# Encoder block in 32-bit floats: three of five units of the down projection by seven products, accumulators of one bank, running sums of squares

## The chip, the cores and the metric

The kernel runs on one core of a Trainium2 chip. The metric is the device time of one execution in microseconds (us); of several runs the median counts.

A core has a matrix engine (TensorE, in profiles PE, its weight loads PEld), a vector engine (VectorE, DVE), a scalar engine (ScalarE, ACT), GpSimd (POOL) and SyncE (SP), which here issues the transfers (DMA). Each engine works through its own list of instructions in order and waits on semaphores for the others. Matmuls write into eight accumulator banks of 128 x 512 floats.

## The reference

One layer of an encoder on x (256 tokens x 2048), all in 32-bit floats, cut to its steps:

```python
hn = rmsnorm(h, mix_norm_pre)
z, xbc, dt_raw, u = split(hn @ w_in)                    # 2048 -> 3616 columns
y_ssd  = ssd_mixer(z, xbc, dt_raw, ...)                 # state space mixer, both directions, 16 heads
y_pool = pool_mixer(u, pool_w, pool_scale)              # means over windows of 2, 4, 8, 16
h = h + rmsnorm(concat(y_ssd, y_pool) @ w_out, mix_norm_post)
hn = rmsnorm(h, ffn_norm_pre)
gate, val = split(hn @ w_up)                            # 2048 -> 2 x 5632
ff = (gelu(dwconv(gate)) * val) @ w_down                # 5632 -> 2048
h = h + rmsnorm(ff, ffn_norm_post)
gate = sigmoid(rmsnorm(h, ple_norm_pre) @ w_gate)       # 2048 -> 2048
h = h + rmsnorm(gate * (p @ w_ple), ple_norm_post)      # p: 256 tokens x 256
```

Every rmsnorm divides a row by the root of its mean square, so the whole row has to be known before the first element of the result.

## The kernel before

**The products.** Each weight tile is loaded raw (four buffers), cast to a rounded high part by ScalarE (`whi`) and subtracted from it by VectorE (`wlo`, the low part); five buffers each. A product of 32-bit floats is then three matmuls: high x high, high x low, low x high. The activations are held in the same two parts, as panels with the channels on the partitions.

**The stages in order.** The first projection columns (dt and u, accumulators `dtu`), then three slabs of `xbc`, then `z`, then w_out (`wo`), then for each of 11 slabs of 512 columns gate (`ga`) and value (`va`), then w_down (`dn`), then w_gate (`gt`). The small product `ple` with w_ple (24 matmuls a half) runs between w_out and gate, and between down and w_gate. Loads are issued by SP in the order of the program; within one engine a scheduler has fixed the order of the instructions when the program was built, so the order that counts is the one shown below under the change.

**Work aside.** While xbc and z run, the mixer's small steps are done in between: `work` holds a list of jobs for each unit of the product, and `aside()` runs the next list at each unit's end. `seg` makes one pair of exponents (two matmuls into two spare banks, a copy by ScalarE, a minimum by VectorE, the exponential by ScalarE); `pool_mix` and `pool_map` are the pooling mixer.

**Down.** The 44 k tiles of w_down are taken in 22 units of two, once for each half of the 2048 output columns. A normal unit is 24 matmuls: two k tiles, two token tiles, two banks of 512 columns, three parts. A unit in `seven` takes the 2 x 2 block product by seven block products, 21 matmuls (`seven_products`). It needs sums of weight blocks (`weight_sums`: f and g, three vector instructions) and of activation blocks (`block_sums`, stored to memory and read back as `sums`, split into `hs`). For some units f and g are made in the value stage and stored (`block_ahead`, read back as `bm`); for the others they are made on the spot. Its names in the profile: `dn014b`, `a`, `c`, `d` are the four split weight sets of the unit with k tiles 14 and 15 in half 0 (unit 7), `dn018f` and `dn018g` sums made on the spot for unit 9. Four of the seven products go into four more banks, `dns`, and `combine` adds those into the normal accumulators `dna` behind the first slow unit after the last fast one.

**The end of a sublayer.** `sublayer` runs w_out and down. Behind each half, for the two token tiles t and two banks n, ScalarE squares the bank with a row sum (`woj`, `dnj`) and VectorE multiplies it by the gain (`wom`, `dnm`). Behind half 1 `rms` adds four row sums of a tile on GpSimd, one after the other, and takes the power −1/2 (`wo0r`, `wo1r`). Then h is updated by VectorE, 512 columns at a time, transposed by TensorE (`woxt`, `dnxt`), and split into the next panel (`wox`; `dnxh`, `dnxl`). `rfj`, `rf0r`, `rfbw`, `rfbp` are the row statistics of the new h for the next stage.

**Accumulators.** Six of the eight banks are three pairs (`pmain`, 128 x 1024), two are single (`pmisc`). `main` and `pair_of_banks` hand out a pair as one tile; a wait for a tile is a wait for both banks. `total` adds the two halves of each bank (high and low parts of gate or value).

Of the kernel before, what the change touches and what calls it, by code (L numbers as in the profile page):

```python
# [51 lines left out]
def build(nc, a, out):  # L52
# [5 lines left out]
    with tile.TileContext(nc) as tc, \  # L58
# [3 lines left out]
            tc.tile_pool(name="small", bufs=1) as sp, \  # L62
            ExitStack() as early, \
            tc.tile_pool(name="dram", bufs=1, space=bass.MemoryType.DRAM) as dp, \
            tc.tile_pool(name="pmain", bufs=3, space=bass.MemoryType.PSUM) as pm, \
            tc.tile_pool(name="pmisc", bufs=2, space=bass.MemoryType.PSUM) as pc:

        def ins(r):
# [2 lines left out]
        def page(name, dtype=F32):  # L71
            return gp.tile([P, 2048], dtype, tag="pg", bufs=14, name=name)
# [5 lines left out]
            return sp.tile([P, n], F32, tag="tiny", bufs=40, name=name)  # L78

        def main(name):  # L80
            t = pm.tile([P, 1024], F32, tag="main", name=name)
            return [t[:, :512], t[:, 512:]]

        def pair_of_banks(name):
            return pm.tile([P, 1024], F32, tag="main", name=name)

        def misc(name):
            return pc.tile([P, 512], F32, tag="misc", name=name)

        def mm(o, lhsT, rhs, start, stop):  # L90
            nc.tensor.matmul(o, lhsT, rhs, start=start, stop=stop, skip_group_check=True)  # L91


        ep = early.enter_context(tc.tile_pool(name="early", bufs=1))
# [16 lines left out]
        for i in range(16):  # L111
            nc.tensor.transpose(warm[:, :P], ident, ident)

        xt = [ep.tile([P, V_SCW + L], F32, name="xt0")] + [page(f"xt{i}") for i in (1, 2)]
        vt = cp.tile([P, V_N - V_SCW], F32, name="vt")
        small = ep.tile([P, 89 + 512], F32, name="small")

# [213 lines left out]
        def feature_pairs(name, w, c0, get, acc):  # L331


            def high(u, tiles):
                for j, (wh, _) in enumerate(tiles):
                    for k, f, s in block(u, j):
                        mm(acc[:, f * 512:(f + 1) * 512], wh[:, s], get.both(k), k == 0, False)

            def low(u, tiles):
                for j, (_, wl) in enumerate(tiles):  # L340
                    for k, f, s in block(u, j):
                        mm(acc[:, f * 512 + L:(f + 1) * 512], wl[:, s], get(k)[0], False, False)
# [12 lines left out]

        def total(o, acc):

            v, w = o.rearrange("p (f t) -> p f t", f=2), acc.rearrange("p (f q t) -> p q f t", f=2, q=2)
            nc.scalar.copy(v, w[:, 1])
            nc.vector.tensor_add(v, v, w[:, 0])  # L360

        def rms(name, parts, scale, n=1, base=EPS):

# [249 lines left out]

        def pool_mix(g):
            ps = misc(f"mx{g}")
            for c in range(2):
                for s, (t0, t1) in enumerate(((0, P + 8), (P - 8, L))):
                    mm(ps[:, c * L + t0:c * L + t1],
                       ut[:, s * 1024 + g * 256 + c * P:s * 1024 + g * 256 + (c + 1) * P],
                       pmat[:, (2 * g + s) * L + t0:(2 * g + s) * L + t1], s == 0, s == 1)  # L620
            nc.vector.tensor_copy(mixt[:, g * 512:(g + 1) * 512], ps)

        def pool_map(g):
# [86 lines left out]
        def job(f, *args):  # L710
# [8 lines left out]
        ])  # L719
        bc = xbc(2)  # L720
        work.extend([
            [job(seg, 0), job(seg, 1), job(pool_map, 0), job(pool_map, 1)],
            [job(seg, 2), job(cb, bc, 0), job(cb, bc, 1)],
            [job(seg, 3), job(seg, 4), job(pool_map, 2)],
            [job(seg, 5), job(pool_map, 3)],
        ])
        xa = xbc(0)
        work.extend([
            [job(seg, 6), job(scale_by_dt, 0, 0, 0)],
            [job(seg, 7), job(scale_by_dt, 0, 0, 1), job(weigh, 0, 0)],  # L730
            [job(xs_turn, xa, 0)],
            [],
        ])
        xb = xbc(1)
        y = page("y")
# [56 lines left out]
        def sublayer(name, w, ks, get, gain, h, vnext, panel=Panel, fast=((), ()), sums=None, hooks={}, base=(EPS, EPS), made=None, ahead=None):  # L792

            mg = [page(f"{name}m{t}") for t in range(2)]
            sq = [[], []]
            for half in range(2):

                alt = main(f"{name}s{half}") if fast[half] and half == 0 else []
                acc = [main(f"{name}a{half}{t}") for t in range(2)]
                if fast[half]:  # L800
                    alt += (main(f"{name}s{half}") if half else []) + [misc(f"{name}s{half}_{i}") for i in (2, 3)]
                token_major(f"{name}{half}", w, half * 1024, ks, get, acc, 1, fast[half], alt, sums,
                            hooks if half else {}, made)
                for t in range(2):
                    for n in range(2):
                        q = tiny(f"{name}q{t}{half}{n}", 1)
                        junk = mid(f"{name}j{t}{half}{n}")[:, :512]
                        c = slice(half * 1024 + n * 512, half * 1024 + (n + 1) * 512)
                        b = acc[t][n]
                        nc.scalar.activation(junk, b, AF.Square, accum_out=q)  # L810
                        nc.vector.tensor_mul(mg[t][:, c], b, gain[:, c])
# [96 lines left out]
        for s in range(DFF // 512):  # L908
            sc = mid(f"gr{s}")
            for i in range(2):  # L910
                ga = pair_of_banks(f"ga{s}{i}")
# [10 lines left out]
            hh, hl = hid[s]  # L922
            hv = mid(f"hv{s}")
            for i in range(2):
                va = pair_of_banks(f"va{s}{i}")
# [159 lines left out]
```

## Time and profile before

| | |
|---|---|
| runs | 1130.02, 1131.77 and 1133.52 us, median 1131.77 |
| profiled execution | 1130.95 us, span 1129.2, mean clock 0.996 |
| TensorE | busy 1112.7 us, 99% of the span |
| VectorE, ScalarE | 798.6 us (71%), 662.1 us (59%) |
| GpSimd | 52.0 us (5%) |
| transfers | 270.4 MB, 239 GB/s in the mean |

Span times of the stages: dt and u up to 52.9 us, xbc up to 144, z up to 199.6, w_out up to 288.4, the change to gate and the first round up to 327, gate and value up to 794, down up to 1021.5, then w_gate up to 1120.3 and the end at 1129.2.

How to read the rows: a group's row gives line, engine, operation, tile written and tiles read, shape, count, then busy time and mean ns of one, then idle time of the engine ahead of it and what ended it. A timeline's row begins with start and duration in us. A row of waits gives who waited for whom, the sum in us, how often, the longest. TensorE's matmuls overlap, so the distance from start to start is their price, not the duration. L91 is the helper that issues every matmul.

### The profile page before, as it was taken

How to read it: one execution, taken by the hardware profiler on the slowest of the kernel's cores; microseconds unless marked ns; L12 is line 12 of the kernel's file. 1: busy time of each engine (PE TensorE's matmuls, PEld its weight loads, DVE VectorE, ACT ScalarE, POOL GpSimd, SP SyncE). 2: the span in 40 equal slices, each digit the busy share in tenths (PEclk: the TensorE clock that was granted, in tenths of full speed). 3: DMA queues.
4: the chain of work that ended last, by engine and by line, in shares of the span. 5: the costliest groups of instructions: out<-in, count | busy, mean ns of one | idle time of the engine just before them, and what ended most of it. 6: DMA issues, size and time to landing. Idle time of an engine off the chain costs nothing.

```text
span 1129.2 us, 15491 instructions
## 1 busy us (share of the span) xinstructions
PE 1112.7 (99%) x6031; PEld 968.1 (86%) x6031; DVE 798.6 (71%) x937; ACT 662.1 (59%) x933; POOL 52.0 (5%) x80
## 2 busy tenths in 40 slices
PE   9999999999899999999999999999999999999996
PEld 9999988888788888888888888888888888887885
DVE  6658877754767777767767676666777778787573
ACT  6747774543675565655656555646656466567462
POOL 0300023100100000000000000000000000001001
PEclk9999999999999999999999999999999999999998
DMA  9944356666577878887797697666788788885742
GB/s 354 385 153 150 114 184 203 234 185 198 187 259 253 270 263 254 264 296 250 254 318 246 224 319 259 196 196 201 258 291 284 251 276 322 302 286 192 238 135 75
DMA packets 143993, 270.43 MB, mean 239 GB/s; under 512 B 5296, under 2 KB 98352, under 8 KB 140592
## 3 DMA queue, kind: packets, MB, share of 16 engines
q1 hardware_dynamic: 143632, 269.09, 71.0%
q8 instruction: 47, 0.77, 0.3%
q10 hardware_dynamic: 288, 0.36, 0.1%
q14 instruction: 26, 0.21, 0.1%
HBM read 247.93 MB, written 21.50 MB: 239 GB/s over the span
## 4 chain that ended last, share of the span: by engine, by line
PE 92%; DVE 3%; ACT 3%; DMA 1%; issue 1%; POOL 1%; POOLq 0%; DVEq 0%; ACTq 0%
PE va L91 22%; PE ga L91 21%; PE dna L91 15%; PE woa L91 7%; PE gt L91 7%; PE xbc L91 6%; PE dns L91 5%; PE z L91 4%; PE dtu L91 2%; DMA dtur<-w_in 1%; PE pw L91 1%; PE yd L91 1%; DVE h_back L820 0%; PE seg L91 0%; ACT rxj L395 0%
## 5 line engine op out<-in xcount | busy, mean ns | idle before, releaser
L91 PE MATMUL ga<-wox,ug_0whi 128*128 128x512 f32 x352 | 88.6, 394 | 1.5 <-DVE wox L201 1.5
L91 PE MATMUL va<-wox,uv_0whi 128*128 128x512 f32 x352 | 87.6, 391 | 0.0
L91 PE MATMUL ga<-wox,ug_1whi 128*128 128x512 f32 x352 | 87.5, 390 | 0.0
L91 PE MATMUL va<-wox,uv_1whi 128*128 128x512 f32 x352 | 87.0, 390 | 0.0
L91 PEld LDWEIGHTS va<-wox,uv_1whi 128*128 128x128 f32 x352 | 66.1, 188 | 13.7
L91 PEld LDWEIGHTS ga<-wox,ug_1whi 128*128 128x128 f32 x352 | 66.0, 188 | 13.6
L91 PEld LDWEIGHTS ga<-wox,ug_0whi 128*128 128x128 f32 x352 | 64.9, 190 | 14.0 <-DVE wox L201 1.7
L91 PEld LDWEIGHTS va<-wox,uv_0whi 128*128 128x128 f32 x352 | 64.7, 188 | 12.5
L91 PE MATMUL ga<-wox,ug_1wlo 128*128 128x256 f32 x352 | 50.2, 284 | 0.0
L91 PE MATMUL ga<-wox,ug_0wlo 128*128 128x256 f32 x352 | 49.5, 283 | 0.0
L91 PE MATMUL va<-wox,uv_1wlo 128*128 128x256 f32 x352 | 49.4, 284 | 0.0
L91 PE MATMUL va<-wox,uv_0wlo 128*128 128x256 f32 x352 | 49.3, 283 | 0.0
L91 PEld LDWEIGHTS ga<-wox,ug_0wlo 128*128 128x128 f32 x352 | 46.8, 191 | 1.7
L91 PEld LDWEIGHTS va<-wox,uv_0wlo 128*128 128x128 f32 x352 | 46.7, 191 | 1.7
L91 PEld LDWEIGHTS ga<-wox,ug_1wlo 128*128 128x128 f32 x352 | 45.6, 192 | 0.3 <-ACT wox L200 0.3
L91 PEld LDWEIGHTS va<-wox,uv_1wlo 128*128 128x128 f32 x352 | 45.4, 192 | 0.0
L91 PE MATMUL xbc<-hnh,xb_0whi 128*128 128x256 f32 x96 | 28.1, 293 | 0.2 <-DVE u L539 0.2
L91 PE MATMUL xbc<-hnh,xb_1whi 128*128 128x256 f32 x96 | 27.5, 286 | 0.0
L366 POOL TENSOR_SCALAR dn0m<-dnq,fmean 128x1 f32<-128x1 f32 x1 | 0.3, 264 | 589.9 <-ACT dnj L810 589.9
L91 PE MATMUL xbc<-hnh,xb_0wlo 128*128 128x256 f32 x96 | 27.3, 285 | 0.0
L91 PE MATMUL xbc<-hnl,xb_1whi 128*128 128x256 f32 x96 | 27.2, 283 | 0.0
L91 PE MATMUL xbc<-hnh,xb_1wlo 128*128 128x256 f32 x96 | 27.2, 283 | 0.0
(1427 smaller groups left out, 3016.0 us busy)
## 6 DMA issues: line engine op xcount, KB each, us to landing
dn0r<-w_ffn_down SPq DMA_DIRECT2D x16, 1024.0 KB, 6.8
dn1r<-w_ffn_down SPq DMA_DIRECT2D x15, 1024.0 KB, 6.4
br<-w_ffn_down SPq DMA_DIRECT2D x13, 1024.0 KB, 5.6
bm<-block SPq DMA_DIRECT2D x13, 1024.0 KB, 6.3
zr<-w_in SPq DMA_DIRECT2D x8, 1024.0 KB, 5.3
wo0r<-w_out SPq DMA_DIRECT2D x8, 1024.0 KB, 6.0
wo1r<-w_out SPq DMA_DIRECT2D x8, 1024.0 KB, 5.6
gt0r<-w_ple_gate SPq DMA_DIRECT2D x8, 1024.0 KB, 5.9
```

The source lines that it names most:

```text
L91: nc.tensor.matmul(o, lhsT, rhs, start=start, stop=stop, skip_group_check=True)
L366: nc.gpsimd.tensor_scalar(m, q, scale, base, op0=ALU.mult, op1=ALU.add)
```

## The change

1. `seven` is 1, 3, 5, 6, 8, 10, 11, 13, 15, 16, 18 in place of the odd numbers up to 19: with half 0 one unit short, 10 + 11 fast units in place of 9 + 10. Blocks are made ahead for all but 3, 8, 13 and 18 (14 in place of 13). The combination comes one unit earlier, behind unit 17 and 19.
2. The main accumulators are single banks, six of them; `total` works bank by bank.
3. The sums of squares run along: each bank's row sum is added by GpSimd as soon as it is there, and the power follows a tile's last sum.
4. The exponent pairs are spread, one a unit, over xbc(0) and xbc(1), `pool_map` with them; the pooling matmuls are held behind the last TensorE instruction that stands ahead of them in the program.
5. The x tiles 1 to 8 lie in a raw weight buffer in place of a page.

```diff
-            tc.tile_pool(name="pmain", bufs=3, space=bass.MemoryType.PSUM) as pm, \
+            tc.tile_pool(name="pmain", bufs=6, space=bass.MemoryType.PSUM) as pm, \
...
         def main(name):
-            t = pm.tile([P, 1024], F32, tag="main", name=name)
-            return [t[:, :512], t[:, 512:]]
-
-        def pair_of_banks(name):
-            return pm.tile([P, 1024], F32, tag="main", name=name)
+            return [pm.tile([P, 512], F32, tag="main", name=f"{name}_{i}") for i in range(2)]
...
         def mm(o, lhsT, rhs, start, stop):
-            nc.tensor.matmul(o, lhsT, rhs, start=start, stop=stop, skip_group_check=True)
+            last["pe"] = ins(nc.tensor.matmul(o, lhsT, rhs, start=start, stop=stop, skip_group_check=True))
...
-        xt = [ep.tile([P, V_SCW + L], F32, name="xt0")] + [page(f"xt{i}") for i in (1, 2)]
+        xt = [ep.tile([P, V_SCW + L], F32, name="xt0")] + [wp.tile([P, 2048], F32, tag="raw", bufs=4, name="xt1"), page("xt2")]
...
         def total(o, acc):
-            v, w = o.rearrange("p (f t) -> p f t", f=2), acc.rearrange("p (f q t) -> p q f t", f=2, q=2)
-            nc.scalar.copy(v, w[:, 1])
-            nc.vector.tensor_add(v, v, w[:, 0])
+            for f in range(2):
+                nc.scalar.copy(o[:, f * L:(f + 1) * L], acc[f][:, L:])
+                nc.vector.tensor_add(o[:, f * L:(f + 1) * L], o[:, f * L:(f + 1) * L], acc[f][:, :L])
...
         def pool_mix(g):
             ps = misc(f"mx{g}")
+            behind = last["pe"]
             for c in range(2):
                 for s, (t0, t1) in enumerate(((0, P + 8), (P - 8, L))):
-                    mm(ps[:, c * L + t0:c * L + t1],
...
+                    with tc.issue_after(behind):
+                        mm(ps[:, c * L + t0:c * L + t1],
...
         bc = xbc(2)
         work.extend([
-            [job(seg, 0), job(seg, 1), job(pool_map, 0), job(pool_map, 1)],
+            [job(seg, 0), job(pool_map, 0)],
+            [job(seg, 1), job(pool_map, 1)],
             [job(seg, 2), job(cb, bc, 0), job(cb, bc, 1)],
-            [job(seg, 3), job(seg, 4), job(pool_map, 2)],
-            [job(seg, 5), job(pool_map, 3)],
+            [job(seg, 3), job(pool_map, 2)],
         ])
         xa = xbc(0)
         work.extend([
-            [job(seg, 6), job(scale_by_dt, 0, 0, 0)],
-            [job(seg, 7), job(scale_by_dt, 0, 0, 1), job(weigh, 0, 0)],
-            [job(xs_turn, xa, 0)],
-            [],
+            [job(seg, 4), job(pool_map, 3), job(scale_by_dt, 0, 0, 0)],
+            [job(seg, 5), job(scale_by_dt, 0, 0, 1), job(weigh, 0, 0)],
+            [job(seg, 6), job(xs_turn, xa, 0)],
+            [job(seg, 7)],
         ])
...
             mg = [page(f"{name}m{t}") for t in range(2)]
-            sq = [[], []]
+            mean, r = list(base), []
...
                         nc.vector.tensor_mul(mg[t][:, c], b, gain[:, c])
-                        sq[t].append(q)
+                        m = tiny(f"{name}m{t}{half}{n}", 1)
+                        nc.gpsimd.tensor_scalar(m, q, 1.0 / D, mean[t], op0=ALU.mult, op1=ALU.add)
+                        mean[t] = m
+                    if half:
+                        r.append(tiny(f"{name}r{t}", 1))
+                        nc.gpsimd.tensor_tensor(r[t], mean[t], mhalf[:, :1], op=ALU.pow)
             if ahead:
                 ahead()
-            r = [rms(f"{name}{t}", sq[t], 1.0 / D, 1, base[t]) for t in range(2)]
...
-        seven = list(range(1, 20, 2))
+        seven = [u for u in range(1, 19) if u % 5 in (0, 1, 3)]
         sums = {u: dp.tile([P, 512], F32, name=f"sums{u}") for u in seven}
-        ahead = [(u, half) for u in seven if u % 6 != 3 for half in range(2) if half or u < 19]
+        ahead = [(u, half) for u in seven if u % 5 != 3 for half in range(2)]
```

GpSimd's list at the end of w_out, before (`woq` are row sums, `wo0m` and `wo1m` the sums of tile 0 and 1):

```order
L366 TENSOR_SCALAR wo0m_2692<-woq_2386 128x1
L366 TENSOR_SCALAR wo0m_2694<-woq_2390,wo0m_2692 128x1
L366 TENSOR_SCALAR wo0m_2696<-woq_2676,wo0m_2694 128x1
L366 TENSOR_SCALAR wo0m_2698<-woq_2680,wo0m_2696 128x1
L369 TENSOR_TENSOR wo0r<-wo0m_2698,mhalf 128x1
L366 TENSOR_SCALAR wo1m_2702<-woq_2394 128x1
L366 TENSOR_SCALAR wo1m_2704<-woq_2398,wo1m_2702 128x1
L366 TENSOR_SCALAR wo1m_2706<-woq_2684,wo1m_2704 128x1
L366 TENSOR_SCALAR wo1m_2708<-woq_2688,wo1m_2706 128x1
L369 TENSOR_TENSOR wo1r<-wo1m_2708,mhalf 128x1
```

and now, where `woq_2402` to `woq_2414` belong to half 0 (the first of its four sums, `wom_2400`, stands ahead of these rows), and `woq_2696` to `woq_2716` to half 1:

```order
L811 TENSOR_SCALAR wom_2406<-woq_2402,wom_2400 128x1
L811 TENSOR_SCALAR wom_2412<-woq_2408 128x1
L811 TENSOR_SCALAR wom_2418<-woq_2414,wom_2412 128x1
L811 TENSOR_SCALAR wom_2700<-woq_2696,wom_2406 128x1
L811 TENSOR_SCALAR wom_2706<-woq_2702,wom_2700 128x1
L815 TENSOR_TENSOR wor_2708<-wom_2706,mhalf 128x1
L811 TENSOR_SCALAR wom_2714<-woq_2710,wom_2418 128x1
L811 TENSOR_SCALAR wom_2720<-woq_2716,wom_2714 128x1
L815 TENSOR_TENSOR wor_2722<-wom_2720,mhalf 128x1
```

Tile 1's two sums of half 0 moved from behind the power of tile 0 to ahead of half 1; two sums and a power are left behind each tile. On TensorE the first two transposes (`woxt`) stood behind 22 of the 24 ple matmuls; now they stand behind the last matmul of w_out, then 12 ple matmuls, six transposes, 11 ple matmuls, eight transposes, the last ple matmul and 10 of gate.

VectorE at the same place, before, with the gain products (L811), the updates of h (L820) and splits of gate's first weights (L157):

```order
L157 TENSOR_TENSOR ug_0wlo<-ug00r_2902,ug_0whi 128x1024
L811 TENSOR_TENSOR wom_2074<-woa_2402,gmix 128x512 x2
L157 TENSOR_TENSOR ug_1wlo<-ug00r_2902,ug_1whi 128x1024
L811 TENSOR_TENSOR wom_2075<-woa_2403,gmix 128x512
L157 TENSOR_TENSOR ug_0wlo<-ug00r_2944,ug_0whi 128x1024
L811 TENSOR_TENSOR wom_2075<-woa_2403,gmix 128x512
L820 SCALAR_TENSOR_TENSOR h_2068<-wom_2074,wo0r,h_2068 128x512
L820 SCALAR_TENSOR_TENSOR h_2069<-wom_2075,wo1r,h_2069 128x512
```

and now:

```order
L153 TENSOR_TENSOR ug_0wlo<-ug00r_2919,ug_0whi 128x1024
L809 TENSOR_TENSOR wom_2082<-woa_0_2420,gmix 128x512
L809 TENSOR_TENSOR wom_2082<-woa_1_2421,gmix 128x512
L822 SCALAR_TENSOR_TENSOR h_2076<-wom_2082,wor_2708,h_2076 128x512 x2
L809 TENSOR_TENSOR wom_2083<-woa_0_2422,gmix 128x512
L822 SCALAR_TENSOR_TENSOR h_2076<-wom_2082,wor_2708,h_2076 128x512
L809 TENSOR_TENSOR wom_2083<-woa_1_2423,gmix 128x512
L822 SCALAR_TENSOR_TENSOR h_2077<-wom_2083,wor_2722,h_2077 128x512 x3
```

The updates of tile 0 (`h_2076`) moved ahead of the products of tile 1, and two splits moved behind the updates.

VectorE in down, at the sums made on the spot for unit 8 in half 0 (f and g, L218 and L220), which follow two fast units with blocks made ahead (`dn010`, `dn012`) and stand ahead of the splits of the slow unit 7 (`dn_0wlo`, `dn_1wlo`), now:

```order
L153 TENSOR_TENSOR dn010dwlo<-bm_0_7579,dn010dwhi 128x1024
L153 TENSOR_TENSOR dn012bwlo<-dn0r_7618,dn012bwhi 128x1024
L153 TENSOR_TENSOR dn012awlo<-dn0r_7618,dn012awhi 128x512
L153 TENSOR_TENSOR dn012cwlo<-bm_0_7624,dn012cwhi 128x1024
L153 TENSOR_TENSOR dn012dwlo<-bm_0_7624,dn012dwhi 128x1024
L218 TENSOR_TENSOR dn016f<-dn0r_7699 128x1024
L153 TENSOR_TENSOR dn_0wlo<-dn0r_7665,dn_0whi 128x1024
L153 TENSOR_TENSOR dn_1wlo<-dn0r_7665,dn_1whi 128x1024
L153 TENSOR_TENSOR dn016bwlo<-dn0r_7699,dn016bwhi 128x1024
L153 TENSOR_TENSOR dn016awlo<-dn0r_7699,dn016awhi 128x512
```

and before, for unit 9, behind one fast unit (`dn014`, unit 7) and ahead of the slow unit 8:

```order
L157 TENSOR_TENSOR dn014bwlo<-dn0r_7486,dn014bwhi 128x1024
L157 TENSOR_TENSOR dn014awlo<-dn0r_7486,dn014awhi 128x512
L157 TENSOR_TENSOR dn014cwlo<-bm_0_7492,dn014cwhi 128x1024
L157 TENSOR_TENSOR dn014dwlo<-bm_0_7492,dn014dwhi 128x1024
L222 TENSOR_TENSOR dn018f<-dn0r_7567 128x1024
L224 TENSOR_TENSOR dn018g<-dn0r_7567,dn018f 128x512
L157 TENSOR_TENSOR dn_0wlo<-dn0r_7533,dn_0whi 128x1024
L157 TENSOR_TENSOR dn_1wlo<-dn0r_7533,dn_1whi 128x1024
```

In both, f stands ahead of the slow unit's splits; now two fast units, not one, precede it.

At the end of down TensorE had the ple matmuls behind the last down matmul, 21 in one piece and three earlier, and the transposes of the new h behind them; now two transposes of tile 0 come first, then 14 ple matmuls, six transposes, 10 ple matmuls and one of w_gate.

More of the change, by code (lines that the diff above doesn't have):

```diff
@@ L336, in high @@
                     for k, f, s in block(u, j):
-                        mm(acc[:, f * 512:(f + 1) * 512], wh[:, s], get.both(k), k == 0, False)
+                        mm(acc[f], wh[:, s], get.both(k), k == 0, False)
             def low(u, tiles):
@@ L341, in low @@
                     for k, f, s in block(u, j):
-                        mm(acc[:, f * 512 + L:(f + 1) * 512], wl[:, s], get(k)[0], False, False)
+                        mm(acc[f][:, L:], wl[:, s], get(k)[0], False, False)
             def block(u, j):
@@ L615, in pool_mix @@
             ps = misc(f"mx{g}")
+            behind = last["pe"]
             for c in range(2):
                 for s, (t0, t1) in enumerate(((0, P + 8), (P - 8, L))):
-                    mm(ps[:, c * L + t0:c * L + t1],
-                       ut[:, s * 1024 + g * 256 + c * P:s * 1024 + g * 256 + (c + 1) * P],
-                       pmat[:, (2 * g + s) * L + t0:(2 * g + s) * L + t1], s == 0, s == 1)
+                    with tc.issue_after(behind):
+                        mm(ps[:, c * L + t0:c * L + t1],
+                           ut[:, s * 1024 + g * 256 + c * P:s * 1024 + g * 256 + (c + 1) * P],
+                           pmat[:, (2 * g + s) * L + t0:(2 * g + s) * L + t1], s == 0, s == 1)
             nc.vector.tensor_copy(mixt[:, g * 512:(g + 1) * 512], ps)
@@ L910, in build @@
             for i in range(2):
-                ga = pair_of_banks(f"ga{s}{i}")
+                ga = main(f"ga{s}{i}")
                 feature_pairs(f"ug{s}{i}", w_up, s * 512 + i * 256, hf, ga)
@@ L924, in build @@
             for i in range(2):
-                va = pair_of_banks(f"va{s}{i}")
+                va = main(f"va{s}{i}")
                 feature_pairs(f"uv{s}{i}", w_up, DFF + s * 512 + i * 256, hf, va)
```

## The prediction

> **What bounds the kernel.** I read the engine totals and the chain that ended last, then the windows by stage, then what PE waited for.
>
> ```profile
> PE 1112.7 (99%) x6031; PEld 968.1 (86%) x6031; DVE 798.6 (71%) x937; ACT 662.1 (59%) x933; POOL 52.0 (5%) x80
> PE 92%; DVE 3%; ACT 3%; DMA 1%; issue 1%; POOL 1%; POOLq 0%; DVEq 0%; ACTq 0%
> ...
> 288.40:327.00 38.60, 34.75 (x190) 28.72 (x188) 29.02 (x44) 27.34 (x46) 6.75 (x13) 0.96 0.68 225
> 327.00:794.00 467.00, 467.00 (x2691) 413.79 (x2690) 331.26 (x366) 270.62 (x362) 0.00 (x0) 1.00 0.78 255
> 794.00:1021.50 227.50, 227.44 (x1003) 187.66 (x1002) 178.03 (x185) 134.76 (x159) 1.06 (x4) 1.00 0.81 279
> 1026.30:1040.30 14.00, 13.12 (x71) 10.28 (x71) 11.72 (x22) 10.59 (x22) 0.13 (x1) 1.00 0.60 198
> ...
> PE ga L91 <- DVE wox L201: 1.5, 1, 1.5
> PE woxt L380 <- DVE wox L201: 1.5, 3, 0.8
> PE seg L91 <- ACT E L605: 0.6, 1, 0.6
> PE gt L91 <- DVE gt_1wlo L157: 0.4, 1, 0.4
> PE mx L91 <- ACT u L538: 0.3, 1, 0.3
> PE xbc L91 <- DVE u L539: 0.2, 1, 0.2
> ```
>
> The windows' columns are length, busy time of PE, PEld, DVE, ACT and POOL, then clock, DMA share and GB/s. TensorE is the bound: in gate and value (327–794) and in down (794–1021.5) it is busy all the time, with DVE at 71% and 78% beside it. Time can come off in two ways only: fewer matmuls, or shorter stalls at the changes of stage. The waits above are small, but the first two stand in a stretch (288–327) where the clock was 0.96 too.
>
> **Fewer matmuls in down.** One fast unit, the slow one behind it, and the vector work around them:
>
> ```profile
> 829.80 0.39 PE L91 MATMUL dna<-dn014bwhi,hs 128*128 128x512 f32 x1
> 834.56 0.62 PE L91 MATMUL dna<-dn_0whi,hidh 128*128 128x512 f32 x2
> 835.01 0.62 PE L91 MATMUL dna<-dn_0wlo,hidh 128*128 128x512 f32 x2
> 840.00 0.39 PE L91 MATMUL dna<-dn018bwhi,hs 128*128 128x512 f32 x1
> ...
> 830.94 1.23 DVE L222 TENSOR_TENSOR dn018f<-dn0r 128x1024 f32<-128x1024 f32 x1 [1.35 <-DMA dn0r<-w_ffn_down]
> 832.20 0.69 DVE L224 TENSOR_TENSOR dn018g<-dn0r,dn018f 128x512 f32<-128x512 f32 x1
> 832.81 1.22 DVE L157 TENSOR_TENSOR dn_0wlo<-dn0r,dn_0whi 128x1024 fp32r<-128x1024 f32 x1
> 836.22 0.68 DVE L157 TENSOR_TENSOR dn018awlo<-dn0r,dn018awhi 128x512 fp32r<-128x512 f32 x1
> 837.60 0.69 DVE L157 TENSOR_TENSOR hs<-sums,hs 128x512 fp32r<-128x512 f32 x1
> ```
>
> A fast unit is 834.56 − 829.80 = 4.76 us (21 matmuls, so 0.2267 each), a slow one 840.00 − 834.56 = 5.44 (24). Two more units become fast (19 to 21 over both halves): 6 × 0.2267 = 1.36 us less on PE.
>
> It is a gain only while VectorE keeps up. By these rows a fast unit whose blocks were made ahead needs three 128x1024 splits (1.22) and two of 512 columns (0.69): 5.04 us. A slow one needs 2.44. A fast one with its sums made on the spot adds f and the two halves of g (1.23 + 2 × 0.69 = 2.61): 7.65. Five units now hold two, one and two of these kinds: 10.08 + 7.65 + 4.88 = 22.6 us against 3 × 4.76 + 2 × 5.44 = 25.2 on PE, 90%. Before, six units needed 25.1 of 30.6, 82%. Two fast units in a row (5 and 6, 10 and 11, 15 and 16) fall behind by 0.28 us each, which the slow ones give back. So nothing is lost on average. The risk is the order: f of unit 8 (dn016f) stands on VectorE ahead of both splits of unit 7, as dn018f does above, and there f waited 1.35 us for its load, while the split behind it ended at 834.03 and PE first used it at 835.01: 0.98 us to spare. The same happens now five times behind two fast units in a row or on a tighter queue; I allow 0 to 0.5 us each, so the term lies between −1.4 and +1.1 (−1.4 + 5 × 0.5). I take −1.4, since PE did not stop there in before. The 14th block made ahead is two more sums and two stores under value, which VectorE (71%) and the queues hide; if not, about 2 us.
>
> One-bank accumulators split each total into two copies and two adds. The rows say what halving saves:
>
> ```profile
> L359 ACT COPY gr<-ga 128x512 f32<-128x512 f32 x22 | 12.9, 588 | 15.9 <-PE ga L91 15.9
> L416 ACT ACTIVATE fc<-gr,vt 128x256 f32<-128x256 f32 x44 | 22.0, 499 | 0.0
> L360 DVE TENSOR_TENSOR gr<-gr,ga 128x512 f32<-128x512 f32 x22 | 15.1, 688 | 1.5
> ```
>
> At 0.5 us for 256 columns a total costs ScalarE 0.4 us more and VectorE at most as much: 44 × 0.4 = 18 us each, on engines that idle 196 and 136 us in that window. Nothing on PE. Uncovered it would be some tenths at each of 44 banks' release.
>
> **From w_out to the gate.** Here the new order does its work.
>
> ```profile
> 285.93 0.60 ACT L810 ACTIVATE woj<-woa 128x512 f32<-128x512 f32 x1 [1.73 <-PE woa L91]
> 286.65 0.69 DVE L811 TENSOR_TENSOR wom<-woa,gmix 128x512 f32<-128x512 f32 x1 [1.19 <-ACT woj L810]
> 287.38 0.60 ACT L810 ACTIVATE woj<-woa 128x512 f32<-128x512 f32 x1 [0.76 <-DVE wom L811]
> 286.80 0.27 POOL L366 TENSOR_SCALAR wo0m<-woq,wo0m 128x1 f32<-128x1 f32 x1 [41.87 <-ACT woj L810]
> 288.58 0.57 POOL L369 TENSOR_TENSOR wo0r<-wo0m,mhalf 128x1 f32<-128x1 f32 x1
> 290.42 2.08 POOL L366 TENSOR_SCALAR wo1m<-woq,wo1m 128x1 f32<-128x1 f32 x3
> 292.58 1.10 POOL L369 TENSOR_TENSOR wo1r<-wo1m,mhalf 128x1 f32<-128x1 f32 x1
> 293.72 0.75 DVE L820 SCALAR_TENSOR_TENSOR h<-wom,wo1r,h 128x512 f32<-128x512 f32 x1 [0.45 <-POOL wo1r L369]
> 288.39 0.39 PE L91 MATMUL ple<-ple_0whi,pth 128*128 128x512 f32 x1
> 296.91 1.15 PE L91 MATMUL ga<-wox,ug_0whi 128*128 128x512 f32 x2 [1.51 <-DVE wox L201]
> 327.00 1.30 PE L91 MATMUL va<-wox,uv_0whi 128*128 128x512 f32 x5
> ...
> 297.00:298.00 1.00, 1.00 (x2) 0.34 (x2) 1.00 (x3) 0.75 (x2) 0.00 (x0) 0.51 0.00 0
> 299.00:300.00 1.00, 1.00 (x7) 1.00 (x6) 1.00 (x2) 0.43 (x1) 0.00 (x0) 0.50 0.00 0
> ```
>
> From 288.39 to 327.00 PE took 38.6 us. The work in it: 24 ple matmuls (5.44), 32 transposes at an estimated 0.11 (3.5), 128 gate matmuls (22.2: 327–794 holds 21 such rounds, 467/21) and two small ones (0.4), 31.6 in all. So 7.0 us are lost, of which the half clock (0.51 and 0.50 in the windows) about 1.7. ACT's square and VectorE's product took turns on a pair of banks (0.76 above), the second token tile's four sums ran only after the first tile's (2.08 us and 1.10), and h of that tile came at 293.72. With the half-0 sums done long ago, one sum and one power remain behind each tile: h of tile 0 near 287.8–288.5 and of tile 1 near 291.1, 2.6 us earlier, while 23 of the 24 ple matmuls fill the gaps between transposes. What is late next is VectorE: 8 updates of h, 16 wox and 5 splits, about 20 us in order, and then rfj on ScalarE ahead of rfbp. Walking the new order with these durations I get 0.2 us at the first transposes, 0.3 at the next, about 1.3 at the third tile of transposes, 0.5 behind, and 1.2 at rfbp: 3.5 lost in place of 7.0. Ends: nothing gained to −4.5. I take −2.8, because five small waits on in-order queues rarely all come out as walked.
>
> A rule bears on this. GpSimd's sum took 0.27 at 286.80 and its power 0.57 at 288.58, while VectorE read its product out of the matmuls' accumulators; the power at 292.58 took 1.10 beside the update of h, whose operands all lie in the on-chip memory. The Trainium skill, "GPSIMD Engine Reference", section 1 Specifications, says that GpSimd's interfaces to the on-chip memory are shared with VectorE and contend with vector instructions of two such inputs; the trace agrees by those numbers. In the new order h of tile 0 runs on VectorE just when tile 1's sum and power run. Priced from rows, 1.10 + 1.10 in place of 0.27 + 0.57 puts tile 1's h 1.35 us later, with PE standing at its transposes behind the 12 ple matmuls: this term then falls to −1.4 and the time is 1126.4.
>
> The clock is a second lever here: it fell at about 297.0, when PE had waited 1.5 us for its first gate operands, and came back 3.4 us later. My walk has one wait of 1.3 us in the stretch. If that one draws the half clock again, its 1.7 us come back, the term is −1.1 and the time 1126.7. The Trainium skill, "TensorE: Matmul & The Clock Gate", section What's actually happening, puts both the idle time that halves the clock and the busy time that restores it at one window of about 3.4 us; the trace agrees for the way back, while it shows an idle stretch of half that length ahead of the fall. By the page's figure a wait of 1.3 us alone would not cost it.
>
> **From down to w_gate.**
>
> ```profile
> 1026.46 0.44 PE L380 MATMUL dnxt<-ident,h_back 128*128 128x128 f32 x2
> 1028.24 0.73 PE L91 MATMUL gt<-gt_0whi,dnxh 128*128 128x512 f32 x2 [0.24 <-ACT dnxh L200]
> 1035.37 0.73 PE L91 MATMUL gt<-gt_1wlo,dnxh 128*128 128x512 f32 x2 [0.36 <-DVE gt_1wlo L157]
> ```
>
> The window 1026.3–1040.3 holds 32 transposes and 37 matmuls: 3.5 + 8.4 = 11.9 of 14.0 us, 2.1 lost. In the new order the combination ends a unit (5.44 us) earlier, tile 0's transposes stand right behind the last down matmul (about 0.4 us of waiting) and 24 ple matmuls in two blocks cover tile 1 and the first panel columns: −1.5, between −2.1 and 0.
>
> **The small ones.** The first xbc matmuls no longer stand behind the pooling matmuls and wait for one bank of three: the 0.3 and 0.2 above, with restarts up to 1.0; I take −0.7. One exponent pair a unit removes the 0.6 wait at seg, 0.8 from start to start: −0.7, at worst 0. At the start x's second column tile is cast ahead of two pieces of the first weights: 0 to +0.6, +0.3.
>
> Sum: −1.4 − 2.8 − 1.5 − 0.7 − 0.7 + 0.3 = −6.8. The profiled execution took 1130.95 (span 1129.2), the median of the runs 1131.77, 0.8 above. So 1124.2 for such an execution, 1125.0 as a median.
>
> **Rivals.** (a) The stalls move instead of going: PE stands at the first transposes with all of ple behind it, and at rfbp as before; only the products and a little elsewhere remain, −1 to −3: 1129–1130.5. For it: the ends of three terms are zero, and 0.3–0.6 us waits are within what my walk can miss. Against: h of tile 1 clearly waits for sums that are now done. (b) Slower: f of an on-the-spot unit holds up the slow unit's splits, because two fast units ahead leave VectorE no slack and the queue, at 81% already, lands loads later. There are eight such places; to end 3.4 us slower than before with the other terms as forecast takes 10.2 − 1.4 = 8.8 us or more, 1.1 at each, so f would have to wait 2.1 us past PE's 0.98, 3.4 instead of 1.35. That gives 1135. Against it stands that PE is busy 227.44 of 227.50 us in down.
>
> **How the numbers follow.** All terms about as forecast 0.58, GpSimd contended 0.10, the half clock kept 0.10, rival (a) 0.15, rival (b) 0.07. 0.3% (3.4 us) is about what a measurement of this kernel can tell. The first three are faster (0.78 together), (a) lies within 0.3%, (b) is slower. Low end: all terms at their best (−1.4 − 4.5 − 2.1 − 1.0 − 0.8) give −9.8 and 1122.0; with the 1.5 us that a median may lie off, from runs up to 1.75 us apart from theirs, 1120.5. High end: into (a), 1130.5.
>
> **What would show it.** Right: two fast units' length 4.76 in a row with no PE gap in down and its end 1.4 earlier; the first wor ahead of 288.0; no half clock near 297; value's first matmul near 324; gate's first transposes without gaps over 0.5. Wrong: PE waiting for VectorE's splits behind f; a PE wait over 1 us at woxt, dnxt or rfbp; a clock under 1 again between 288 and 327.

## The result and the profile after

The change took 1125.59 us (median of four runs, 1124.68 to 1126.40) against 1131.68 before: ratio 0.9945, 95% interval 0.993 to 0.996. The forecast was 1125.0, range 1120.5 to 1130.5. A second time, beside other kernels, it took 1125.02 (six runs, 1123.65 to 1128.37; ratio 0.9952, 0.994 to 0.9965).

The totals and the chain of the changed kernel's page, its windows by stage (each from the stage's own first matmul), and what PE waited for:

```profile
PE 1108.6 (99%) x6025; PEld 966.2 (86%) x6025; DVE 807.3 (72%) x997; ACT 670.9 (60%) x983; POOL 48.3 (4%) x80
PE 96%; ACT 1%; issue 1%; DVE 0%; POOL 0%; DMA 0%; SPq 0%; DVEq 0%; POOLq 0%; ACTq 0%
...
288.49:323.81 35.32, 33.39 (x191) 27.69 (x189) 27.85 (x44) 26.96 (x46) 3.74 (x9) 1.00 0.70 240
323.81:790.57 466.76, 466.76 (x2690) 413.44 (x2689) 334.68 (x415) 273.15 (x404) 0.00 (x0) 1.00 0.79 260
790.57:1015.65 225.08, 225.08 (x994) 186.25 (x992) 185.47 (x197) 140.15 (x168) 2.77 (x8) 1.00 0.84 289
...
PE woxt L376 <- DVE wox L197: 1.1, 2, 0.9
PE dtu L87 <- ACT dtu0whi L152: 0.8, 1, 0.8
PE pw L87 <- ACT E L601: 0.6, 1, 0.6
PE rfbp L87 <- DVE rfbw L402: 0.5, 1, 0.5
```

The half clock between w_out and value is gone (1.00 in the first window), value's first matmul comes at 323.81, and PE did not stop once in down. But two waits are new: `pw` for an exponent pair where `seg` waited before, and `dtu` at the start. From first and last matmuls of the two traces, what each stretch gave:

| stretch (us) | before | change | difference | forecast |
|---|---|---|---|---|
| start to dtu's last matmul | 52.38 | 53.62 | +1.24 | +0.3 |
| dtu's last to xbc's first | 1.81 | 0.51 | −1.30 | −0.7 |
| xbc's first to w_out's first | 145.23 | 145.61 | +0.38 | −0.7 |
| w_out's last to value's first | 38.84 | 35.32 | −3.52 | −2.8 |
| gate and value | 466.8 | 466.8 | 0.0 | 0 |
| down, first to last | 227.51 | 224.85 | −2.66 | −1.4 |
| down's last to w_gate's last | 98.72 | 98.05 | −0.67 | −1.5 |
| w_gate's last to the end | 9.18 | 9.42 | +0.24 | 0 |

Three ple matmuls (0.68 us) that stood inside down before stand behind it now, so the two last big rows read −1.98 and −1.35. Of the −1.98, six matmuls are 1.36, and 0.47 are small stops at the combination in half 0 (891.2) and early in half 1 (914.8) that no longer happen; the fifth experiment shows that single banks alone remove those.

The sum came out. The experiments ask whether for the reasons given: the running sums at w_out's end, the units, the jobs.

### The profile page after: what moved, and what is told of

It is laid out like the page before. It is cut to its first block, busy times and chain, and to the rows that moved or that the text cites. A ratio compares the mean times of both kernels' runs of the same rounds, so it can differ in the third digit from the quotient of the medians.

```text
span 1122.9 us, 15604 instructions
## 1 busy us (share of the span) xinstructions
PE 1108.6 (99%) x6025; PEld 966.2 (86%) x6025; DVE 807.3 (72%) x997; ACT 670.9 (60%) x983; POOL 48.3 (4%) x80
## 4 chain that ended last, share of the span: by engine, by line
PE 96%; ACT 1%; issue 1%; DVE 0%; POOL 0%; DMA 0%; SPq 0%; DVEq 0%; POOLq 0%; ACTq 0%
PE va L87 22%; PE ga L87 21%; PE dna L87 15%; PE woa L87 8%; PE gt L87 7%; PE xbc L87 6%; PE dns L87 5%; PE dtu L87 4%; PE z L87 4%; PE pw L87 1%; PE yd L87 1%; PE ple L87 0%; PE mx L87 0%; DMA xt<-x_cols 0%; PE dnxt L376 0%
## 5 line engine op out<-in xcount | busy, mean ns | idle before, releaser
L87 PE MATMUL xbc<-hnl,xb_0whi 128*128 128x256 f32 x96 | 27.1, 282 | 0.0
```

Of the source, the lines that this page charges most:

```text
L87: last["pe"] = ins(nc.tensor.matmul(o, lhsT, rhs, start=start, stop=stop, skip_group_check=True))
```

## The experiments

Read below: stretch A, from w_out's last matmul to value's first (38.84 before, 35.32 with the change); stretch B, from down's last to w_gate's last (98.72, 98.05); down from first to last.

**1 to 4. Banks or sums.** Two parts, each there or not. First, the change with pairs of banks again:

```diff
-            tc.tile_pool(name="pmain", bufs=6, space=bass.MemoryType.PSUM) as pm, \
+            tc.tile_pool(name="pmain", bufs=3, space=bass.MemoryType.PSUM) as pm, \
...
-            return [pm.tile([P, 512], F32, tag="main", name=f"{name}_{i}") for i in range(2)]
+            t = pm.tile([P, 1024], F32, tag="main", name=name)
+            return [t[:, :512], t[:, 512:]]
```

> The changed kernel with accumulators as pairs of banks again; the running sums stay. Read: from w_out's last matmul to value's first, 38.84 us before, 35.32 with the change. Theory (the banks carry it: a square no longer waits for the pair's other bank nor takes turns with the product, so h of both tiles is ready 0.7 to 1 us earlier and the scheduler puts ple between the transposes): 37.5 to 38.5. Rival (the running sums carry it): 35.3 to 36. From down's last matmul to w_gate's last, 98.72 before and 98.05 now with three more ple matmuls (0.68) in it: theory 98.8 to 99.3, rival 98.0.

Measured: 1134.59 in a single run, 4.2 over the kernel before beside it (1130.42). A was 39.39, longer than either theory gave, B 99.48. The half clock was back in A (0.50 from 301.6 to 305.0). Four of PE's waits:

```profile
PE woxt L377 <- DVE wox L198: 2.4, 2, 1.3
PE dna L88 <- DVE dna L245: 1.5, 1, 1.5
PE xbc L88 <- DVE u L536: 1.0, 1, 1.0
PE z L88 <- DVE z_0wlo L154: 0.6, 1, 0.6
```

Second, the change with the sums at the end:

```diff
-                        m = tiny(f"{name}m{t}{half}{n}", 1)
-                        nc.gpsimd.tensor_scalar(m, q, 1.0 / D, mean[t], op0=ALU.mult, op1=ALU.add)
-                        mean[t] = m
...
+                        sq[t].append(q)
             if ahead:
                 ahead()
+            r = [rms(f"{name}{t}", sq[t], 1.0 / D, 1, base[t]) for t in range(2)]
```

> The changed kernel with the four sums of each tile and the power at the end again; one-bank accumulators stay. Same two stretches, 35.32 and 98.05 with the change. Theory (banks): 35 to 36 and 98 to 98.5, since tile 1's two old sums still fit into GpSimd's idle time between tile 0's power (287.97) and tile 1's last row sum (290.0). Rival (sums): 37 to 38.8 and 98.8 to 99.4.

Measured: 1123.36. A was 34.28, under both expected ranges and 1.0 shorter than with the change; B 98.21. Third, both undone:

> Both of these parts undone, the rest of the change stays (units, jobs, x tiles). Either theory: 38.4 to 39.0 from w_out's last matmul to value's first, with the half clock near 297 back, and 99.2 to 99.8 from down's last matmul to w_gate's last. If the stretch stays under 37, something else in the change carries the gain.

Measured: 1132.14; A 37.86, a little under the range, B 99.63. The half clock expected near 297 did not come back. Fourth, the kernel before with running sums alone:

> The kernel before with the running sums alone. Theory (banks): 37.5 to 38.5 from w_out's last matmul to value's first; rival (sums): 35.5 to 36.5. Total: theory 0.3 to 1.5 us under the kernel before, rival 3 to 4 us under it.

Measured: 1130.35 against 1130.42, a smaller gain than either side expected; A 38.00, B 99.39. Stretch A in the kernel before, the first, the third and the fourth experiment (the third figure from the end is the clock):

```profile
288.16:327.00 38.84, 34.99 (x191) 28.92 (x189) 29.26 (x44) 27.58 (x46) 6.92 (x13) 0.96 0.67 224
...
290.53:329.92 39.39, 35.24 (x191) 29.03 (x189) 28.66 (x44) 26.85 (x47) 4.34 (x11) 0.96 0.65 222
...
290.89:328.75 37.86, 33.58 (x191) 27.83 (x189) 28.56 (x44) 27.07 (x47) 6.93 (x13) 1.00 0.69 231
...
287.80:325.80 38.00, 33.84 (x191) 27.73 (x190) 29.07 (x44) 27.52 (x46) 4.34 (x11) 1.00 0.67 231
```

So the banks carry A: going from pairs to single ones takes it from 37.86 to 34.28 with the clock full in both, and with running sums from 39.39 to 35.32. Running sums lengthen it by 1.0 with single banks, again with the clock full in both. With pairs their effect stays open: A is 1.5 longer in the first experiment than in the third, and 0.8 shorter in the fourth than in the kernel before (where B grows by 0.7), but each time the longer of the two had the half clock, which the prediction priced at about 1.7. The rows of the change, and behind the break those of the kernel with the sums at the end (w_out's last matmul at 288.49 and 287.41):

```profile
287.40 0.57 POOL L815 TENSOR_TENSOR wor<-wom,mhalf 128x1 f32<-128x1 f32 x1
288.00 1.42 DVE L822 SCALAR_TENSOR_TENSOR h<-wom,wor,h 128x512 f32<-128x512 f32 x2 [0.39 <-POOL wor L815]
290.03 0.78 POOL L811 TENSOR_SCALAR wom<-woq,wom 128x1 f32<-128x1 f32 x1 [1.15 <-ACT woj L808]
290.90 0.56 POOL L815 TENSOR_TENSOR wor<-wom,mhalf 128x1 f32<-128x1 f32 x1
291.49 2.08 DVE L822 SCALAR_TENSOR_TENSOR h<-wom,wor,h 128x512 f32<-128x512 f32 x3 [0.21 <-POOL wor L815]
292.30 0.88 PE L376 MATMUL woxt<-ident,h 128*128 128x128 f32 x6 [0.28 <-DVE h L822]
300.06 0.63 PE L376 MATMUL woxt<-ident,h 128*128 128x128 f32 x4 [0.91 <-DVE wox L197]
311.87 0.46 PE L87 MATMUL rfbp<-ident,rfbw 128*128 128x128 f32 x2 [0.54 <-DVE rfbw L402]
...
287.26 0.62 POOL L362 TENSOR_SCALAR wo1m<-woq,wo1m 128x1 f32<-128x1 f32 x2
289.31 0.29 POOL L362 TENSOR_SCALAR wo1m<-woq,wo1m 128x1 f32<-128x1 f32 x1 [1.43 <-ACT woj L808]
290.64 0.74 DVE L818 SCALAR_TENSOR_TENSOR h<-wom,wo1r,h 128x512 f32<-128x512 f32 x1
290.83 0.41 PE L376 MATMUL woxt<-ident,h 128*128 128x128 f32 x2
298.05 0.63 PE L376 MATMUL woxt<-ident,h 128*128 128x128 f32 x4 [0.41 <-DVE wox L197]
```

Tile 1's h starts 3.0 us behind w_out's last matmul with running sums (291.49) and 3.2 without (290.64): the old sums of tile 1 run while GpSimd would idle before its last row sum (1.43). Before, it was 5.6 behind (293.72 after 288.16). Most of the 2.3 us comes from the squares, which wait for their own bank only: the last one started 2.75 us behind w_out's last matmul before (290.91), and 0.70 behind it in both kernels here. What running sums change is an order. Tile 0's power ends 0.5 us ahead of w_out's last matmul in both kernels, but with running sums VectorE's list has the first updates of tile 0's h ahead of tile 1's products (288.00, against 289.99 without), and TensorE's list has its transposes first and the next ones in eights; PE then stands for both spare banks to be emptied (0.91 in the row, and 0.18 behind it). With the sums at the end they come in fours between gate matmuls, with waits of 0.41 and 0.36.

**5 to 7. What the parts are worth in time.** The kernel before with one-bank accumulators and nothing else:

> The kernel before with one-bank accumulators alone: old units, sums at the end, old jobs, x tiles in a page. Theory (the banks carry nearly all but the products): 34.0 to 35.5 from w_out's last matmul to value's first (38.84 before), no stop behind the combination in down, total 1124 to 1126.5. Rival (the parts are needed together): stretch over 36.5, total 1127 to 1129.5.

Measured: 1124.03 (1123.48 to 1124.22) against 1130.50, ratio 0.9941 (0.9929 to 0.9954), as much as the whole change. A 34.35, dtu's last to xbc's first 0.52, down 226.21 without a stop, B 98.86. With the new units added:

```diff
-        seven = list(range(1, 20, 2))
+        seven = [u for u in range(1, 19) if u % 5 in (0, 1, 3)]
...
-        ahead = [(u, half) for u in seven if u % 6 != 3 for half in range(2) if half or u < 19]
+        ahead = [(u, half) for u in seven if u % 5 != 3 for half in range(2)]
```

> One-bank accumulators and the new units; sums at the end, old jobs, x tiles in a page. Theory: 1.4 us (six matmuls at 0.2267) under the kernel with the banks alone, 1122.5 to 1125, and 0.5 to 2.5 under the whole change (1125.59), because the running sums cost 1.0 at w_out's end and the new jobs 0.8 in xbc. Rival (sums or jobs or x tiles gain somewhere else): 1125.5 or more.

Measured: 1123.61 (1121.95 to 1123.81), ratio 0.9933 (0.9921 to 0.9946): 0.4 under the banks alone, where 1.4 was expected. Down took 226.21 again, with 1.3 us of stops, so what it gained lies behind down (B 98.20). The first stop, on VectorE and on PE, and behind the break what ScalarE waited for ahead of the second (PE at 959.93):

```profile
934.72 1.23 DVE L218 TENSOR_TENSOR dn116f<-dn1r 128x1024 f32<-128x1024 f32 x1 [2.25 <-DMA dn1r<-w_ffn_down]
935.86 1.22 DVE L153 TENSOR_TENSOR dn_0wlo<-dn1r,dn_0whi 128x1024 fp32r<-128x1024 f32 x1
937.14 0.73 PE L87 MATMUL dna<-dn_0wlo,hidh 128*128 128x512 f32 x2 [0.45 <-DVE dn_0wlo L153]
...
956.27 0.62 ACT L152 CAST hs<-sums 128x512 fp32r<-128x512 f32 x1 [2.56 <-DMA sums<-sums]
```

The first is rival (b)'s place: f waited 2.25 us for its load, and the slow unit's split behind it was late for PE. The second is not: there ScalarE's cast of stored sums waited 2.56 us for its load, with the casts of unit 11 behind it. The kernel of the second experiment, timed:

> The changed kernel with the sums at the end, the same program as in the second run above, now timed. Theory (running sums cost 1.0 at w_out's end and gain nothing at down's): 1124.0 to 1125.0. Rival (the 1.4 us in that look were the start's clock): 1125.3 to 1126.

Measured: 1123.37 (1122.67 to 1124.77), ratio 0.994 (0.9926 to 0.9954). Under the expected range by 0.6; the intervals of all these overlap with the change's, so that the sums cost 1.0 is read from stretch A, which was 35.31 to 35.35 in all four profiles with single banks and running sums and 34.28 to 34.35 in all six with sums at the end.

**8. Where VectorE becomes the bound.** Four of five units fast:

```diff
-        seven = [u for u in range(1, 19) if u % 5 in (0, 1, 3)]
+        seven = [u for u in range(1, 19) if u % 5 != 2]
...
-        ahead = [(u, half) for u in seven if u % 5 != 3 for half in range(2)]
+        ahead = [(u, half) for u in seven if u % 5 in (0, 1) for half in range(2)]
```

> The changed kernel with four of five units fast, 27 in place of 21; blocks made ahead for the same units, units 4, 9 and 14 on the spot too. PE alone would need 18 matmuls less, 4.1 us, down 220.8 us. VectorE per five units by durations 2 x 5.04 + 2 x 7.65 + 2.44 = 27.8 against 24.5 on PE: down about 240 and slower by 10 or more. By starts (1.14 and 0.60 in place of 1.22 and 0.69): 25.4 against 24.5, down 222 to 226 with stops of PE at each on-the-spot unit. Rival (VectorE is no bound yet): 221 to 221.5.

Measured: 1132.68, down 232.59. The window over down, and four of PE's waits in it:

```profile
790.72:1023.54 232.82, 227.65 (x976) 180.44 (x974) 212.55 (x234) 150.94 (x187) 2.89 (x8) 1.00 0.80 282
...
PE dns L87 <- DVE dn026dwlo L153: 0.6, 1, 0.6
PE dns L87 <- ACT dn128dwhi L152: 0.5, 1, 0.5
PE dns L87 <- DVE dn018dwlo L153: 0.5, 1, 0.5
PE dns L87 <- DVE dn118cwlo L153: 0.4, 1, 0.4
```

VectorE is busy 91% (212.55 of 232.82; 82% with the change), and PE loses 11 us in small pieces from start to start, mostly at the c and d sets of on-the-spot units. Both sums of mine missed, 222 to 226 by starts and 240 by durations. That waits between ScalarE's casts and VectorE's splits fill the difference is my reading of the rows; no run separates it. Eighteen matmuls less turned into 7.7 us more.

**9 to 11. f, held back.** The change again, then banks and units with f behind the slow unit's splits, then banks and units again, on one chip.

> The change itself, unaltered, beside the next two on the same chip. If the sums cost 1.0 at w_out's end and the jobs 0.3 in xbc, its median lies 1 to 2 us over theirs and its stretch from w_out's last matmul to value's first is 35.3 again. If it lies within 0.5 of them, what the stretch loses comes back elsewhere. Its start is also a second look at the clock: dtu's last matmul near 52.3 if the late 53.6 was chance, near 53.6 if the order of x's second column tile makes it.

Measured: 1125.02, against 1121.88 and 1123.50 for the next two. A 35.35, down 224.90 without a stop in this profile, dtu's last matmul at 52.21: the late 53.62 was not the order alone.

```diff
                     two = ready.pop(name) if u == 0 and name in ready else split_two(name, w, k0, c0)
+                    last["slow"] = last["dve"]
...
+            with tc.issue_after(behind) if behind else nullcontext():
-            nc.vector.tensor_sub(f.rearrange("p (b c) -> p b c", b=2), v[:, 1:3],
+                nc.vector.tensor_sub(f.rearrange("p (b c) -> p b c", b=2), v[:, 1:3],
...
```

Here `behind` is `last["slow"]`, taken in `seven_products` and handed to `weight_sums`.

> Banks and new units (sums at the end, old jobs, x tiles in a page), with f of a sum made on the spot held on VectorE behind the slow unit's two splits. Theory (f, waiting for its load, holds up the slow unit's split behind it, and gives back the matmuls saved): down's stretch 224.9 to 225.3 in place of 226.2, no stop of PE at a dn_0 split, total about 1 us under the next kernel. Rival (late loads stop PE wherever f stands): 225.8 or more, with the stop moved to a fast unit's own sets.

Measured: 1121.88 in four runs from 1121.51 to 1122.27, ratio 0.9919 (0.9906 to 0.9931): the fastest here, and below the change in the same session (0.994 to 0.9965). Down 224.87 with no stop.

> Banks and new units again, unaltered, to see how far down's stretch (226.2 in the first look, 225.1 without any stop) varies with the loads. Theory: between 224.9 and 226.5, with stops at other places than 936 and 959 if the landing of loads decides; at the same places by the same amounts if the order alone does.

Measured: 1123.50, six runs from 1121.96 to 1126.83. The profile is of the slowest of them, and down took 229.80, beyond the range. Its rows, then VectorE's in the same place with f behind the splits (tenth experiment):

```profile
848.71 1.23 DVE L218 TENSOR_TENSOR dn026f<-dn0r 128x1024 f32<-128x1024 f32 x1 [4.18 <-DMA dn0r<-w_ffn_down]
849.85 1.22 DVE L153 TENSOR_TENSOR dn_0wlo<-dn0r,dn_0whi 128x1024 fp32r<-128x1024 f32 x1
851.12 0.74 PE L87 MATMUL dna<-dn_0wlo,hidh 128*128 128x512 f32 x2 [2.37 <-DVE dn_0wlo L153]
852.00:855.00 3.00, 3.00 (x9) 2.33 (x8) 3.00 (x5) 0.00 (x0) 0.00 (x0) 0.51 0.57 175
...
844.94 1.22 DVE L153 TENSOR_TENSOR dn_0wlo<-dn0r,dn_0whi 128x1024 fp32r<-128x1024 f32 x1
850.22 1.22 DVE L219 TENSOR_TENSOR dn026f<-dn0r 128x1024 f32<-128x1024 f32 x1
```

One load that came late held f for 4.18 us; the split behind it needed only data that was there. PE stopped for 2.5 us, and the clock then fell to 0.51 for some 3 us more. In the tenth experiment the same load was late too (ScalarE's cast of it waited until 847.39), but the splits had started at 844.94 and PE did not stop. The stops came at 937 and 960 in the sixth experiment's profile, at 851 in this one, of the same program: the loads' landing decides where.

**12. f held back in the whole change.**

> The whole change with f held behind the slow unit's splits, nothing else altered. The change's own runs lay between 1123.65 and 1128.37. Theory (that spread is f waiting for its load): runs within 1.5 us of each other, median 1123 to 1124.5, down's stretch 224.9 to 225.1. Rival (the spread comes from the start's clock or elsewhere): spread 3 us or more, median 1124.5 to 1126.

Measured: 1125.05, runs from 1123.61 to 1126.66, ratio 0.9951 (0.9938 to 0.9965): no gain, and the spread stays at 3 us. The rival came true. So f alone is not what makes the change's runs differ, and the tenth kernel's lead is not f's alone: sums at the end, the old jobs and the page go with it, and these were not separated further. The profile shows the largest stop in down, of the same kind on another engine, ScalarE:

```profile
859.97 0.62 ACT L152 CAST hs<-sums 128x512 fp32r<-128x512 f32 x1 [2.65 <-DMA sums<-sums]
860.50 1.05 ACT L152 CAST dn_0whi<-dn0r 128x1024 fp32r<-128x1024 f32 x1
862.86 0.73 PE L87 MATMUL dna<-dn_0wlo,hidh 128*128 128x512 f32 x2 [0.53 <-DVE dn_0wlo L153]
```

The cast of the stored sums stands ahead of the slow unit's cast and waited 2.65 us for its load. This is the commoner kind: the stops in the second (947.8) and seventh (959.7) experiment, and the sixth's second, also lie behind such a cast, which had waited 2.56 to 2.67 us. And the start was late (dtu's last matmul at 53.99). The start of the change, and PE's speed behind it in the change and in the ninth run:

```profile
5.21 0.51 ACT L196 ACTIVATE hnh<-xt,xt 128x256 fp32r<-128x256 f32 x1 [0.60 <-DMA xt<-x_cols]
6.15 1.93 PE L87 MATMUL dtu<-dtu0whi,hnh 128*128 128x352 f32 x5 [0.80 <-ACT dtu0whi L152]
7.00:9.50 2.50, 2.50 (x10) 2.50 (x10) 2.19 (x5) 1.95 (x5) 0.00 (x0) 1.00 1.02 392
...
7.00:9.50 2.50, 2.50 (x18) 2.50 (x17) 2.19 (x5) 1.72 (x5) 0.00 (x0) 1.00 0.97 379
```

At this stop PE's matmuls lie 1.40 to 1.60 us apart from start to start in all eight profiles with x's tiles in a weight buffer (0.70 to 0.83 in the six with a page). In three of the eight (the change's first profile, the eighth and the twelfth) matmuls then ran at half their rate, 10 instead of 18 in this window, until 9.6 to 10.3 us, and dtu ended at 53.6 to 54.0; in the other five, and in all with a page, it ended at 51.8 to 52.7. Whether a page alone would settle the change's spread was not tried.

## Why the prediction was right, and where it was not

**The total** came from a sum whose terms missed in both directions.

**Fewer matmuls:** the size (1.36) and the cover hold in the change's two profiles, where down took 224.85 and 224.90 without a stop. The allowance of 0 to 0.5 us at each f named a real mechanism; taking its best end was the choice that failed, since of the other profiles with these units and single banks four lost 0.6 to 1.3 us in stops, half to nearly all of what six matmuls save, and one 4.8; only the tenth, with f held back, lost nothing. That "PE did not stop there in before" rested on one profile. The working counts five such places; there are eight, as its rival (b) has it. Rival (b) named one place; its price is paid by chance, at one place in a run and not at eight. The other place, the cast of stored sums on ScalarE, had no term, and four of the six larger stops lie there. The 14th block and the split totals cost nothing on PE: gate and value took 466.8 in both.

**From w_out to the gate:** my walk of the new order gave 3.5 lost, and the trace has 35.32 − 31.6 = 3.7; the shading to −2.8 was not needed. That the two agree so well is partly luck. From start to start the five places lost 0.1, 0.4, 1.1, 0.4 and 0.7 us, 2.7 in all, where 0.2, 0.3, 1.3, 0.5 and 1.2 were walked; the other 1.0 lies in matmuls and transposes that cost more than the 31.6 allows. One sign named there failed: the wait of 0.91 us at 300.06 is over the 0.5 allowed at gate's first transposes. The step that failed is its reason, "with the half-0 sums done long ago". Tile 1's h is early by the banks. The bank part stood in that paragraph as a remark (ACT and VectorE taking turns) and was not priced by itself; priced from 0.76 of turns at two tiles it would have been seen as a term.

**GpSimd contended:** of tile 1's two sums the first took 0.54 and the second 0.78, where 0.27 had been measured, the power 0.56: 0.5 us of the 1.35 priced in the last sum. Both sums ran beside updates of h (288.00 and 289.94), as the rule of the Trainium skill, "GPSIMD Engine Reference", section 1 Specifications, has it; the power ran beside a product and was not slowed. **Half clock:** waits of 1.1 and 0.4 in the stretch did not draw it here. A wait of 1.3 us is not harmless in general, though: in the first experiment waits of 0.8 and 1.3 us close together did draw it (301.6).

**Down to w_gate:** −1.35 after the ple matmuls are counted, −1.5 foretold. The banks are the larger part: with the new units B is 99.63 with pairs (third experiment) and 98.21 with single banks (second). The units add to it only with single banks: old units have 98.86 there (fifth), new ones 98.20 (sixth).

**The small ones:** the entry to xbc was undervalued: with single banks the bank that xbc needs is freed by a part of dtu that ends early, and there is no wait (−1.3). The jobs failed: spread pairs did not remove the wait, `pw` now stands where the second pair stood, for the same copy behind ScalarE's casts, and the stretch to w_out is 0.3 to 0.7 longer than with the old jobs (145.27); no run separates them from the x tiles and the held pooling matmuls there. With pairs of banks it is 2.2 longer (147.4), which explains part of experiments 1 and 3. The start was sized at +0.3 and can be +1.5.

## What to carry to other kernels

Give each accumulator bank its own tile where one engine reads it while the next is still written: here that alone was worth 0.59% (0.46 to 0.71), as much as five edits together. On an in-order engine ask of each instruction that waits for a load what stands behind it that has its data already. Here such a wait cost nothing in some profiles of the same program and 2.5 us of stop in another, so one profile need not show it. When several edits are priced together, undo them one at a time before believing which of them paid.

## What the hardware showed that was not expected

The half rate at the start shows in the distances of the matmuls (0.29 and 0.16 us at 352 columns), while the clock reads 1.00 in both windows above. The reason is that the trace has no clock record that early: its first, of full clock, comes at 9.58 us in the change's first profile, 9.91 in the eighth and 10.30 in the twelfth, just where the distances halve, and at 4.2 to 7.3 in the other eleven.

Later changes of the clock lie on one grid with that first record, in steps of 3.413 us. In the kernel before the clock fell at 297.01 and came back at 300.43, 85 and 86 steps behind 6.88. In the first experiment it was 301.60 and 305.01, 87 and 88 steps behind 4.64; in the eleventh 852.07 and 855.49, 248 and 249 steps behind 5.57.

What decides seems to be PE's idle time within one step, and not the length of a single stop. In the steps ahead of these three falls PE stood idle for 1.8, 2.0 and 2.4 us. In all fourteen profiles no step with up to 1.75 us was followed by a fall. A single stop of 1.5 us drew the half clock in the kernel before (295.4 to 296.9) but not in the third experiment (298.1 to 299.6), where it fell across two steps, with 1.2 and 1.4 us idle in them. At the start a step with up to 0.64 us idle brought the full clock, and none with 0.74 or more did. So the longer stop at the start, 0.74 to 0.80 us of idle time in the three late profiles, cost a whole step at half rate when it came ahead of the first full clock, and nothing of the kind in the five profiles that had full clock before it. The idle times rest on modelled ends of matmuls, and no run was made to test this reading.

The Trainium skill, "TensorE: Matmul & The Clock Gate", section What's actually happening, explains the chance with a window that runs freely; the grid agrees with it. It gives a whole idle window as what halves the clock, and there the measurement differs: 1.8 us in a step of 3.4 were enough.
